# Down projection of a hybrid decoder layer: Strassen's seven products in place of the plain product

## The chip, the core and the metric

The kernel runs on one core of a Trainium2 chip. The metric is the device time of one execution in microseconds; lower is better. The engines are TensorE (PE for its matmuls, PEld for its weight loads in the profile), VectorE (DVE), ScalarE (ACT), GpSimd (POOL) and SyncE (SP, whose queue issues most of the DMAs).

## The reference

One layer of a hybrid trunk: two attention mixers, an output projection, and a SwiGLU feed-forward. Sequence 2048, width 1024, feed-forward width `D_FF` 2816, all in float32. The change is in the last product and the norm behind it:

```python
h = rmsnorm(x, g_ffn[l])
act = jax.nn.silu(jnp.einsum('bsd,df->bsf', h, w_gate[l])) * jnp.einsum('bsd,df->bsf', h, w_up[l])
x = x + jnp.einsum('bsf,fd->bsd', act, w_down[l])
...
return rmsnorm(x, g_final)
```

## The kernel before

The program has three stretches: the two mixers, then `phase3` with `project_out` (output projection and norm), `ffn_in` (gate and up) and `ffn_out` (down and final norm). The 2048 rows are `NT` = 4 token tiles of 512. A float32 operand is split in two: `hi` is the value cast to the type fp32r by ScalarE, `lo` the difference, taken by VectorE or GpSimd. A product of two operands is three matmuls (hi·hi, hi·lo, lo·hi).

`ffn_in` already uses Strassen's (Winograd's) seven products per block of gate and of up, and stores the activations by DMA in the scratch tensor `sc.act`. `ffn_out` does the plain product: for each token tile `t` and each half `hf` of the 1024 output columns it goes over `NF` = 22 chunks of 128 along `D_FF`. Per chunk there are 4 row blocks and 3 matmuls each, accumulated in four PSUM banks (`dn`). Weights are loaded and split two chunks at a time (`wraw_d`, `wh_d`, `wl_d`), the activations of a tile once for both halves (`actr`, `act`). At the end of a half the banks are added to the residual `xs` (L1162).

The order of instructions within each engine is set when the program is built, by a scheduler that knows estimated durations; on the chip each engine works through its list in order and waits on semaphores. Tiles come from pools that are stacked in SBUF; a tile laid over an older one waits for that one's last reader.

Of the kernel before, what the change touches and what calls it, by code (L numbers as in the profile page):

```python
# [113 lines left out]
def bcast_row(nc, dst, row):  # L114
    nc.sync.dma_start(dst, row.partition_broadcast(P))
# [669 lines left out]
def phase3(tc, consts, x, w_o, g_ffn, w_gate, w_up, w_down, g_final, out, sc):  # L785
    nc = tc.nc
    with ExitStack() as es:
        ps = es.enter_context(tc.tile_pool(name="ps3", bufs=8, space=PSUM, reuse_waits="tile"))
        rw = es.enter_context(tc.tile_pool(name="rw3", bufs=4, reuse_waits="tile"))
        project_out(tc, consts, ps, rw, x, w_o, g_ffn, sc)  # L790
        ffn_in(tc, ps, rw, w_gate, w_up, sc)
        ffn_out(tc, consts, ps, rw, w_down, g_final, out, sc)


def row_rstd(nc, sp, half, src, name):
    sq = sp.tile([P, D], F32, tag="sqr", name="sqr")
    ss = sp.tile([P, 1], F32, tag="ssr", name="ssr")
    nc.scalar.activation(sq, src, AF.Square, accum_out=ss)
    return rstd_of(nc, sp, ss, D, 1, half, name), sq


def project_out(tc, consts, ps, rw, x, w_o, g_ffn, sc):
# [4 lines left out]
    wov = w_o[0].rearrange("(k p) n -> p k n", p=P)  # L807
    with ExitStack() as es:
        pool = lambda name, bufs: es.enter_context(tc.tile_pool(name=name, bufs=bufs, reuse_waits="tile"))
        op, wp0, slot, xp, hp, wp1, cp, sp = (pool(n, b) for n, b in (  # L810
            ("op", 2), ("wo30", 1), ("slot", 6), ("x3", 2), ("hst", 2), ("wo31", 1), ("c3", 1), ("s3", 2)))
        wp = (wp0, wp1)
        gf = cp.tile([P, D], F32, name="gf")
        wo = {}
# [123 lines left out]
def ffn_in(tc, ps, rw, w_gate, w_up, sc):  # L938
# [2 lines left out]
    nc = tc.nc  # L941
    views = [w[0].rearrange("(k p) n -> p k n", p=P) for w in (w_gate, w_up)]
    with ExitStack() as es:
        gp = es.enter_context(tc.tile_pool(name="g3", bufs=1, reuse_waits="tile"))
        tp = es.enter_context(tc.tile_pool(name="t3", bufs=1, reuse_waits="tile"))
        ap = es.enter_context(tc.tile_pool(name="a3", bufs=1, reuse_waits="tile"))
        whl = es.enter_context(tc.tile_pool(name="whl3", bufs=9, reuse_waits="tile"))
        bufs = {"T": 6, "u": 5, "v": 3, "g": 6}
# [133 lines left out]
        for t2 in range(NT // 2):  # L1082
            w0 = weights(views[0], 0, "g")
            S = operands(t2)
            for j in range(DFF // (2 * P)):
                gate = {}

                def gated(a, b, v, psum):
                    g = tmp("g", "gate") if psum else v
                    nc.scalar.activation(g, v, AF.Silu)  # L1090
                    gate[a, b] = g

                def upped(a, b, v, psum):
                    g = gate[a, b]
                    (nc.vector if psum else nc.gpsimd).tensor_mul(g, v, g)  # L1095
                    nc.sync.dma_start(sc.act[2 * t2 + a, :, 2 * j + b, :], g)

                if j:
                    quads(S, views[0], j, "g", "g", gated)
                else:  # L1100
                    first_quads(S, w0, "g", gated)
                quads(S, views[1], j, "u", "v", upped)


def ffn_out(tc, consts, ps, rw, w_down, g_final, out, sc):
    nc = tc.nc
    half = consts[1]
    orr = out[0].rearrange("(i r) d -> r i d", r=16)
    wdv = w_down[0].rearrange("(k p) n -> p k n", p=P)
    NF = DFF // P  # L1110
    with ExitStack() as es:
        actp = es.enter_context(tc.tile_pool(name="act", bufs=29, reuse_waits="tile"))
        whl = es.enter_context(tc.tile_pool(name="wd3", bufs=4, reuse_waits="tile"))
        xp = es.enter_context(tc.tile_pool(name="x4", bufs=1, reuse_waits="tile"))
        sp = es.enter_context(tc.tile_pool(name="s4", bufs=2, reuse_waits="tile"))
        cp = es.enter_context(tc.tile_pool(name="c4", bufs=1, reuse_waits="tile"))
# [3 lines left out]
        def load_act(t, f):  # L1120

            raw = rw.tile([P, 2, 512], F32, tag="raw", name="actr")
            nc.sync.dma_start(raw, sc.act[t, :, f:f + 2, :])
            out = []
            for u in range(2):
                a = actp.tile([P, 2, 512], F32R, tag="act", name="act")
                nc.scalar.copy(a[:, 0], raw[:, u])  # L1127
                nc.gpsimd.tensor_sub(a[:, 1], raw[:, u], a[:, 0].bitcast(F32))  # L1128
                out.append(a)
            return out  # L1130

        def load_w(f, hf):
            raw = rw.tile([P, 2, 512], F32, tag="raw", name="wraw_d")
            nc.sync.dma_start(raw, wdv[:, f:f + 2, hf * 512:(hf + 1) * 512])
            wh = whl.tile([P, 2, 512], F32R, tag="wh", name="wh_d")
            nc.scalar.copy(wh, raw)  # L1136
            wl = whl.tile([P, 2, 512], F32R, tag="wl", name="wl_d")
            nc.vector.tensor_sub(wl, raw, wh.bitcast(F32))  # L1138
            return wh, wl

        def half_out(t, xs, acts, hf, tail):
            acc = [ps.tile([P, 512], F32, tag="mm", name="dn") for _ in range(4)]
            w = {}

            def step(kk, i):
                for n, (a, b) in enumerate(((0, 0), (0, 1), (1, 0))):
                    nc.tensor.matmul(acc[i], acts[kk][:, a, i * P:(i + 1) * P], w[kk // 2][b][:, kk % 2, :],  # L1147
                                     start=(kk == 0 and n == 0), stop=(kk == NF - 1 and n == 2))

            for kk in range(NF):  # L1150
                if kk % 2 == 0:
                    w[kk // 2] = load_w(kk, hf)
                if len(acts) <= kk:
                    acts += load_act(t, kk)
                if kk < NF - tail:
                    for i in range(4):
                        step(kk, i)
            for i in range(4):
                for kk in range(NF - tail, NF):
                    step(kk, i)  # L1160
                xv = xs[:, i, hf * 512:(hf + 1) * 512]
                nc.vector.tensor_add(xv, acc[i], xv)  # L1162

        def final(t, xs):
            for i in range(4):
                rs, y = row_rstd(nc, sp, half, xs[:, i, :], f"z{t}_{i}")
                nc.vector.scalar_tensor_tensor(y, xs[:, i, :], rs, gfin, op0=ALU.mult, op1=ALU.mult)
                nc.gpsimd.dma_start(orr[RES[4 * t + i]], y)

        def half_squares(xs, hf, name):  # L1170
            sq = sp.tile([P, D], F32, tag="sqr", name="sqh")
            ss = sp.tile([P, 4], F32, tag="ssh", name="ssh" + name)
            for i in range(4):
                nc.scalar.activation(sq[:, :512], xs[:, i, hf * 512:(hf + 1) * 512], AF.Square, accum_out=ss[:, i:i + 1])
            return ss

        def final_last(t, xs, s0):
            s1 = half_squares(xs, 1, "1")
            for i in range(4):
                ss = sp.tile([P, 1], F32, tag="ssr", name="ssl")  # L1180
                nc.vector.tensor_add(ss, s0[:, i:i + 1], s1[:, i:i + 1])  # L1181
                rs = rstd_of(nc, sp, ss, D, 1, half, f"zl{i}")
                y = sp.tile([P, D], F32, tag="sqr", name="yl")
                for hf in range(2):
                    cols = slice(hf * 512, (hf + 1) * 512)
                    nc.vector.scalar_tensor_tensor(y[:, cols], xs[:, i, cols], rs, gfin[:, cols], op0=ALU.mult, op1=ALU.mult)  # L1186
                    nc.sync.dma_start(orr[RES[4 * t + i]][:, cols], y[:, cols])

        for t in range(NT):
            last = t == NT - 1  # L1190
            xs = xp.tile([P, 4, D], F32, tag="xs", name=f"xo{t}")
            nc.sync.dma_start(xs, sc.x1[t])
            acts = []
            half_out(t, xs, acts, 0, 0)
            if last:
                s0 = half_squares(xs, 0, "0")
            half_out(t, xs, acts, 1, 4 if last else 0)
            if last:
                final_last(t, xs, s0)
            else:  # L1200
                final(t, xs)
# [31 lines left out]
```

## Time and profile before

| | |
|---|---|
| time, median of 3 runs | 2465.59 us (2462.58 to 2466.73) |
| time of the profiled execution | 2461.11 us |
| its span, first to last instruction | 2459.3 us |
| matmuls of `ffn_out` | 1968.97 us to 2450.40 us of the span |

A page of the profile gives busy time per engine, and can be asked for windows of time, groups of instructions by line, waits, and single instructions in order of time. A wait names the engine that waits and what ended the wait. A busy PE means that matmuls are queued back to back; the granted clock says at which of two speeds they run.

### The profile page before, as it was taken

Reading aid. Unit: us, or ns where it says so; the run is one execution under the profiler, and the core shown is the slowest. Engines: PE = TensorE matmul, PEld = TensorE weight load, DVE = VectorE, ACT = ScalarE, POOL = GpSimd, SP = SyncE. Lnnn points to the kernel's source line nnn. Section 1 sums busy time; section 2 is a strip of 40 time slices with the busy share of each in tenths; the row PEclk is TensorE's granted clock in tenths of the full one; section 3 lists DMA queues with packets and bytes.
Section 4 is the critical chain, followed back from the end, with each engine's and each line's share of the span. In section 5 each row is a group of like instructions: output and inputs, shape, how many; then the busy total and the mean of one; then the engine's idle time right before and its main releaser. Section 6 shows DMA issues by size and latency. Waiting matters only on the chain. (4 is left out here: it accounts for less than half of the span.)

```text
span 2459.3 us, 33676 instructions
## 1 busy us (share of the span) xinstructions
PE 2357.3 (96%) x12029; PEld 1999.6 (81%) x12029; DVE 1441.7 (59%) x2969; ACT 1028.2 (42%) x2361; POOL 460.6 (19%) x431
## 2 busy tenths in 40 slices
PE   7999999998999898989999999899999999999998
PEld 7987788887999776867888887688888778888887
DVE  5335554447999867669565556956655333434342
ACT  5323355554898943344332333433332232323241
POOL 2211211112111021122111012311101151414140
PEclk9999999998999899999999999999999999999999
DMA  7666566569997887843222222322222273636361
GB/s 220 210 189 209 163 180 180 145 171 245 221 221 174 240 230 202 261 159 125 86 86 86 70 95 81 126 90 88 86 69 86 71 254 120 239 122 230 127 231 60
DMA packets 250136, 384.26 MB, mean 156 GB/s; under 512 B 19681, under 2 KB 148321, under 8 KB 244465
## 3 DMA queue, kind: packets, MB, share of 16 engines
q1 hardware_dynamic: 244784, 367.03, 49.7%
q0 software_dynamic: 4896, 14.75, 2.0%
q8 instruction: 95, 1.56, 0.3%
q14 instruction: 73, 0.59, 0.1%
q10 hardware_dynamic: 288, 0.33, 0.0%
HBM read 263.43 MB, written 118.62 MB: 155 GB/s over the span
## 5 line engine op out<-in xcount | busy, mean ns | idle before, releaser
L1147 PE MATMUL dn<-wh_d,act 128*128 128x512 f32 x1408 | 435.2, 390 | 2.3 <-ACT act L1127 2.3
L1147 PEld LDWEIGHTS dn<-wh_d,act 128*128 128x128 f32 x1408 | 264.9, 188 | 58.0 <-ACT act L1127 2.7
L1138 DVE TENSOR_TENSOR wl_d<-wraw_d,wh_d 128x1024 fp32r<-128x1024 f32 x88 | 138.5, 1580 | 272.1 <-ACT wh_d L1136 272.1
L1147 PE MATMUL dn<-wl_d,act 128*128 128x512 f32 x704 | 275.1, 391 | 0.5 <-DVE wl_d L1138 0.5
L1095 POOL TENSOR_TENSOR c<-c,c 128x512 f32<-128x512 f32 x66 | 103.1, 1564 | 714.2 <-DVE c L1041 525.5
L988 ACT CAST wh<-T 128x512 fp32r<-128x512 f32 x176 | 108.9, 624 | 257.3 <-PE Yg L1023 70.7
L468 DVE TENSOR_TENSOR hl<-pt,hl 128x512 fp32r<-128x512 f32 (+1 forms) x224 | 145.2, 657 | 77.4 <-ACT hl L467 76.9
L443 ACT ACTIVATE p<-t,m 128x256 f32<-128x256 f32 (+1 forms) x384 | 176.8, 477 | 18.9 <-DVE m L668 18.9
L1128 POOL TENSOR_TENSOR act<-actr,act 128x512 fp32r<-128x512 f32 x88 | 123.5, 1424 | 255.5 <-ACT act L1127 255.3
L169 PE MATMUL acc<-hh,wh 128*128 128x512 f32 x416 | 170.2, 409 | 0.7 <-DVE vt L239 0.7
L169 PE MATMUL acc<-hh,wl 128*128 128x512 f32 x416 | 170.5, 410 | 0.0
L169 PE MATMUL acc<-hl,wh 128*128 128x512 f32 x416 | 170.2, 409 | 0.0
L885 PE MATMUL acco<-woh,oT 128*128 128x512 f32 x512 | 162.9, 396 | 1.0 <-DVE oT L857 1.0
L1136 ACT CAST wh_d<-wraw_d 128x1024 fp32r<-128x1024 f32 x88 | 91.9, 1049 | 164.3 <-PE dn L1147 143.4
L1147 PEld LDWEIGHTS dn<-wl_d,act 128*128 128x128 f32 x704 | 132.6, 188 | 28.3 <-DVE wl_d L1138 0.9
L486 PE MATMUL o<-hl,v 128*128 128x128 f32 (+1 forms) x816 | 143.3, 297 | 7.6 <-DVE hl L468 6.9
L467 ACT CAST hl<-pt 128x512 fp32r<-128x512 f32 (+1 forms) x224 | 124.8, 565 | 46.3 <-PE pt L462 45.9
L990 DVE TENSOR_TENSOR wl<-T,wh 128x512 fp32r<-128x512 f32 x176 | 122.9, 702 | 32.6 <-ACT wh L988 32.2
L462 PE MATMUL pt<-ident,p 128*128 128x128 f32 x848 | 135.7, 283 | 4.6 <-ACT p L443 2.1
L421 PE MATMUL s<-k,q 128*128 128x256 f32 (+1 forms) x768 | 122.1, 290 | 18.5 <-DMA k<-kB 8.7
L486 PEld LDWEIGHTS o<-hl,v 128*128 128x128 f32 x816 | 113.3, 196 | 11.8 <-DVE hl L468 10.4
L421 PEld LDWEIGHTS s<-k,q 128*128 128x128 f32 x768 | 100.8, 192 | 26.4 <-DVE nma L558 7.1
(453 smaller groups left out, 5509.9 us busy)
## 6 DMA issues: line engine op xcount, KB each, us to landing
wraw_d<-in_w_down_dram SPq DMA_DIRECT2D x88, 512.0 KB
wraw_g<-in_w_gate_dram SPq DMA_DIRECT2D x44, 512.0 KB
wraw_u<-in_w_up_dram SPq DMA_DIRECT2D x44, 512.0 KB
actr<-actS SPq DMA_DIRECT2D x44, 512.0 KB
actS<-c SPq DMA_DIRECT2D x68, 256.0 KB
k<-kB SPq DMA_DIRECT2D x32, 512.0 KB
xt<-in_x_dram SPq DMA_DIRECT2D x16, 512.0 KB
qA<-hia SPq DMA_DIRECT2D x32, 256.0 KB
```

Of the source, the lines that this page charges most:

```text
L169: nc.tensor.matmul(acc, a[:, k, :], mv, start=(n == 0), stop=(n == 3 * KC - 1))
L421: nc.tensor.matmul(s[:, i, :n], b["q"], b["k"][m], start=(m == 0), stop=(m == 1))
L443: nc.scalar.activation(b["pv"](p[:, i, :n]), b["tv"](b["t"]), AF.Exp, scale=-1.0, bias=nm[:, c:c + 1], accum_out=l[:, c:c + 1])
L462: nc.tensor.transpose(pt[:, sl, :], p[:, i, hfn * P:(hfn + 1) * P], ident)
L467: nc.scalar.copy(hi, pt[:, a:z, :])
L468: nc.vector.tensor_sub(lo, pt[:, a:z, :], hi.bitcast(F32))
L486: nc.tensor.matmul(out, v[:, vi, :], mov, start=(first and n == 1), stop=(last and n == 2 * len(jobs)))
L885: nc.tensor.matmul(acc, oT[kk // 2][:, kk % 2, a, i * P:(i + 1) * P], b[:, kk, :], start=(n == 0), stop=(n == 11))
L990: nc.vector.tensor_sub(lo, src, hi.bitcast(F32))
L1128: nc.gpsimd.tensor_sub(a[:, 1], raw[:, u], a[:, 0].bitcast(F32))
L1138: nc.vector.tensor_sub(wl, raw, wh.bitcast(F32))
L1147: nc.tensor.matmul(acc[i], acts[kk][:, a, i * P:(i + 1) * P], w[kk // 2][b][:, kk % 2, :], start=(kk == 0 and n == 0), stop=(kk == NF - 1 ...
```

## The change

`ffn_out` is written anew. Token tiles are taken in two pairs (`t2`), chunks in eleven pairs (`j`), output columns in two halves, so that each pair of chunks is a two by two block product, done with seven products P1 to P7 instead of eight. The eleven pairs form three groups of 4, 4 and 3; a step is one product over one group, so there are 2·3·7 = 42 steps. Each `Pair` loads tile `E` (even chunk: two activation tiles, two weight halves) and `F` (odd chunk). `operands` forms the sums of a product in place in `E`, `F` and `ST` and splits them into `o4` (tag `o`, six buffers): the activation half and the weight half side by side. `self.alt` is VectorE for even `j` and GpSimd for odd `j`.

PSUM holds three sets of four banks, X, Y and Z, out of eight banks; a later product of a set accumulates upon the earlier one, and after every step `evict` adds the set to the residual `xs`, or P1's to `a1`. At the last group the sums with `a1`, the squares and the final norm follow row block by row block. While PE does step `s`, the program lists the operands of step `s + 1` and the evictions of step `s - 1`.

The pools of `project_out`, `ffn_in` and `ffn_out` are opened in another order, so that other tiles lie upon each other, and the last four stores of activations in `ffn_in` go through GpSimd's queue instead of SyncE's.

```diff
-        op, wp0, slot, xp, hp, wp1, cp, sp = (pool(n, b) for n, b in (
-            ("op", 2), ("wo30", 1), ("slot", 6), ("x3", 2), ("hst", 2), ("wo31", 1), ("c3", 1), ("s3", 2)))
+        op, wp0, wp1, cp, sp, xp, hp, slot = (pool(n, b) for n, b in (
+            ("op", 2), ("wo30", 1), ("wo31", 1), ("c3", 1), ("s3", 2), ("x3", 2), ("hst", 2), ("slot", 6)))
...
+                    q = nc.gpsimd if t2 == NT // 2 - 1 and j == DFF // (2 * P) - 1 else nc.sync
+                    q.dma_start(sc.act[2 * t2 + a, :, 2 * j + b, :], g)
...
+    GROUPS = [range(0, 4), range(4, 8), range(8, 11)]
+    ORDER = ("P1", "P6", "P2", "P7", "P5", "P4", "P3")
...
+    BANK = {"P1": "X", "P2": "X", "P6": "Y", "P7": "Y", "P4": "Y", "P5": "Z", "P3": "Z"}
+    TO = {"P6": (0, 1), "P2": (0, 0), "P7": (1, 1), "P5": (1, 1), "P4": (1, 0), "P3": (0, 1)}
...
+        ep, fp, op, st, xp, cp, sp = (pool(n, b) for n, b in (
+            ("e4", 5), ("f4", 4), ("op4", 6), ("st4", 4), ("x4", 3), ("c4", 1), ("s4", 2)))
...
+            def split(self, src, lo):
+                o = op.tile([P, 2, 2, 512], F32R, tag="o", name="o4")
+                nc.scalar.copy(o[:, 0], src)
+                lo.tensor_sub(o[:, 1], src, o[:, 0].bitcast(F32))
+                return o
...
+                if n == "P1":
+                    o = self.split(two(self.E, 0, 3), V)
+                    self.alt.tensor_sub(two(self.E, 1, 3), two(self.E, 0, 2), two(self.E, 1, 3))
+                elif n == "P6":
+                    self.ST = st.tile([P, 2, 512], F32, tag="st", name="ST")
+                    self.alt.tensor_sub(self.ST, two(self.F, 1, 3), two(self.E, 1, 3))
+                    o = self.split(self.ST, V)
+                elif n == "P2":
+                    o = self.split(two(self.F, 0, 2), self.alt)
+                    V.tensor_sub(two(self.F, 0, 2), two(self.F, 0, 2), self.ST)
+                elif n == "P7":
+                    G.tensor_sub(self.E[:, 2], self.F[:, 3], self.E[:, 2])
+                    o = self.split(self.E[:, 1:3], V)
+                elif n == "P5":
+                    G.tensor_add(self.E[:, 0], self.E[:, 0], self.ST[:, 0])
+                    o = self.split(two(self.E, 0, 3), V)
+                elif n == "P4":
+                    o = self.split(self.F[:, 1:3], V)
+                else:
+                    o = self.split(two(self.F, 0, 3), V)
...
+            if n == "P1":
+                if g:
+                    V.tensor_add(a1[t2][:, i], src, a1[t2][:, i])
+                else:
+                    nc.scalar.copy(a1[t2][:, i], src)
+                return
+            a, hf = TO[n]
+            d = xs[t2, a][:, i, hf * 512:(hf + 1) * 512]
+            V.tensor_add(d, src, d)
+            if not end:
+                return
+            add_a1 = {"P6": (0, 1, G), "P2": (1, 1, V), "P7": (1, 0, V)}.get(n)
...
+            def cell(n, bank, ops, kk, i):
+                for m, (u, v) in enumerate(((0, 0), (0, 1), (1, 0))):
+                    nc.tensor.matmul(bank[i], ops[kk][:, u, 0, i * P:(i + 1) * P], ops[kk][:, v, 1, :],
...
+            def other(q):
+                if nxt and q < len(pairs[nxt[:2]]):
+                    made.append(pairs[nxt[:2]][q].operands(nxt[2]))
+                if s:
+                    evict(*steps[s - 1], q)
...
+            for q in range(4):
+                if q < len(ops):
+                    for i in range(4):
+                        cell(n, fresh, ops, q, i)
+                other(q)
+            banks[BANK[n]] = fresh
```

VectorE's list before, at the end of the first half of tile 0. `wl_d` are weight splits, `xo0<-dn` evictions.

```order
L1138 TENSOR_TENSOR wl_d_19226<-wraw_d_19222,wh_d_19224 128x1024
L1138 TENSOR_TENSOR wl_d_19256<-wraw_d_19252,wh_d_19254 128x1024
L1162 TENSOR_TENSOR xo0_18760<-dn_18762,xo0_18760 128x512
L1162 TENSOR_TENSOR xo0_18760<-dn_18763,xo0_18760 128x512
L1162 TENSOR_TENSOR xo0_18760<-dn_18764,xo0_18760 128x512
L1162 TENSOR_TENSOR xo0_18760<-dn_18765,xo0_18760 128x512
L1138 TENSOR_TENSOR wl_d_19286<-wraw_d_19282,wh_d_19284 128x1024
```

VectorE's list now, from P3's step of the first group into P1's of the second. L1148 is the lo part of a split, L1154 and L1157 are sums in place, L1205 evictions.

```order
L1148 TENSOR_TENSOR o4_19301<-E_19112,o4_19301 128x1024
L1157 TENSOR_TENSOR ST_19360<-F_19256,E_18828 128x1024
L1148 TENSOR_TENSOR o4_19318<-E_19116,o4_19318 128x1024
L1148 TENSOR_TENSOR o4_19335<-E_19120,o4_19335 128x1024
L1154 TENSOR_TENSOR E_19116<-E_19116 128x2x512
L1205 TENSOR_TENSOR xo00_18808<-bZ_19124,xo00_18808 128x512
L1157 TENSOR_TENSOR ST_19396<-F_19264,E_19116 128x1024
L1148 TENSOR_TENSOR o4_19362<-ST_19360,o4_19362 128x1024
L1205 TENSOR_TENSOR xo00_18808<-bZ_19125,xo00_18808 128x512
L1205 TENSOR_TENSOR xo00_18808<-bZ_19126,xo00_18808 128x512
L1205 TENSOR_TENSOR xo00_18808<-bZ_19127,xo00_18808 128x512
```

Where an eviction of a half stood behind 11 weight splits, evictions now come every four to eight sums or splits, and the first two sums of the next product stand ahead of them.

GpSimd's list before, at the final norm of tile 0 (L1128 splits of activations, L110 the power of the norm, L1168 stores).

```order
L1128 TENSOR_TENSOR act_19728<-actr_19726,act_19728 128x512
L1128 TENSOR_TENSOR act_19731<-actr_19726,act_19731 128x512
L110 TENSOR_TENSOR rs_z0_0_19531<-ms_z0_0_19529,half_81 128x1
L110 TENSOR_TENSOR rs_z0_1_19540<-ms_z0_1_19538,half_81 128x1
L1168 DMA out_0_dram<-sqr_19526 128x1024
L1168 DMA out_0_dram<-sqr_19535 128x1024
```

GpSimd's list now, at the final norm of tile 1, in which the second pair of tiles has begun.

```order
L110 TENSOR_TENSOR rs_z011_20287<-ms_z011_20285,half_81 128x1
L1157 TENSOR_TENSOR ST_20452<-F_20231,E_20097 128x1024
L1163 TENSOR_TENSOR E_20097<-F_20231,E_20097 128x512
L1166 TENSOR_TENSOR E_20093<-E_20093,ST_20422 128x512
L110 TENSOR_TENSOR rs_z012_20316<-ms_z012_20314,half_81 128x1
L1166 TENSOR_TENSOR E_20097<-E_20097,ST_20452 128x512
L110 TENSOR_TENSOR rs_z013_20333<-ms_z013_20331,half_81 128x1
L1148 TENSOR_TENSOR o4_20503<-F_20223,o4_20503 128x1024
```

The power of the norm, which stood behind two splits of 512, now stands between sums of 1024 and 512 that themselves wait for loads and for VectorE.

## Rows read from the trace of the kernel before

**Rows 1.** The page, busy time by engine over the whole span.

```profile
PE 2357.3 (96%) x12029; PEld 1999.6 (81%) x12029; DVE 1441.7 (59%) x2969; ACT 1028.2 (42%) x2361; POOL 460.6 (19%) x431
```

**Rows 2.** Windows: from:to, length, busy by engine (count), granted clock, DMA share, GB/s.

```profile
1969.00:2450.00 481.00, 480.54 (x2111) 397.39 (x2112) 175.71 (x150) 153.40 (x211) 139.77 (x115) 1.00 0.51 173
2100.00:2120.00 20.00, 20.00 (x90) 16.54 (x90) 10.81 (x9) 9.42 (x14) 11.42 (x11) 1.00 0.94 336
1966.00:1972.00 6.00, 3.73 (x12) 2.41 (x10) 4.04 (x3) 2.18 (x4) 4.58 (x4) 0.78 0.69 246
1972.00:1978.00 6.00, 6.00 (x26) 4.96 (x26) 0.00 (x0) 0.00 (x0) 3.71 (x3) 0.93 0.99 406
```

**Rows 3.** Groups by line, 1850 to 2460 us: busy, mean ns | idle before.

```profile
L1147 PE MATMUL dn<-wh_d,act 128*128 128x512 f32 x1408 | 435.2, 390 | 2.3 <-ACT act L1127 2.3
L1147 PE MATMUL dn<-wl_d,act 128*128 128x512 f32 x704 | 275.1, 391 | 0.5 <-DVE wl_d L1138 0.5
L1138 DVE TENSOR_TENSOR wl_d<-wraw_d,wh_d 128x1024 fp32r<-128x1024 f32 x88 | 138.5, 1580 | 272.1 <-ACT wh_d L1136 272.1
L1136 ACT CAST wh_d<-wraw_d 128x1024 fp32r<-128x1024 f32 x88 | 91.9, 1049 | 164.3 <-PE dn L1147 143.4 <-DMA wraw_d<-in_w_down_dram 8.3 <-PE Yu L1023 5.5
```

**Rows 4.** PE's waits, 1300 to 2459 us: total, times, longest.

```profile
PE dn L1147 <- ACT act L1127: 2.3, 1, 2.3
PE dn L1147 <- DVE wl_d L1138: 0.5, 1, 0.5
```

**Rows 5.** Single lines of the stage: duration in ns, minimum/median/maximum.

```profile
L1138 DVE TENSOR_TENSOR wl_d<-wraw_d,wh_d x88: 1211/1226/2304, 1967.4 to 2429.8; 128x1024 fp32r<-128x1024 f32 x88
L1162 DVE TENSOR_TENSOR xo<-dn,xo x32: 674/691/692, 2029.5 to 2450.8; 128x512 f32<-128x512 f32 x32
L1128 POOL TENSOR_TENSOR act<-actr,act x88: 1274/1296/2318, 1969.7 to 2375.8; 128x512 fp32r<-128x512 f32 x88
```

**Rows 6.** VectorE in order of time: start, duration, instruction, count.

```profile
1091.52 1.89 DVE L990 TENSOR_TENSOR wl<-T,wh 128x512 fp32r<-128x512 f32 x3
...
1108.96 1.79 DVE L967 TENSOR_TENSOR S2l<-s,S2h 128x512 fp32r<-128x512 f32 x1
1110.67 1.78 DVE L967 TENSOR_TENSOR S1l<-s,S1h 128x512 fp32r<-128x512 f32 x1
1112.38 1.78 DVE L967 TENSOR_TENSOR S3l<-s,S3h 128x512 fp32r<-128x512 f32 x1
```

**Rows 7.** GpSimd in order of time, the same stretch.

```profile
1108.46 1.74 POOL L967 TENSOR_TENSOR A12l<-hraw,A12h 128x512 fp32r<-128x512 f32 x1 [3.10 <-ACT A12h L966]
1110.16 1.74 POOL L967 TENSOR_TENSOR A22l<-hraw,A22h 128x512 fp32r<-128x512 f32 x1
1111.87 1.74 POOL L977 TENSOR_TENSOR s<-hraw 128x512 f32<-128x512 f32 x1
```

**Rows 8.** GpSimd in order of time, 878 to 890 us.

```profile
879.13 9.91 POOL L824 TENSOR_TENSOR wol<-wraw_o,woh 128x1024 fp32r<-128x1024 f32 x4 [92.21 <-ACT woh L823]
```

**Rows 9.** VectorE in order of time, the same stretch.

```profile
883.86 2.92 DVE L848 TENSOR_TENSOR ob<-ob 128x512 f32<-128x512 f32 x1 [5.02 <-DMA ob<-oA]
...
889.51 0.68 DVE L848 TENSOR_TENSOR ob<-ob 128x512 f32<-128x512 f32 x1
```

**Rows 10.** PE in order of time, where `ffn_out` begins.

```profile
1966.31 0.39 PE L1023 MATMUL Zu<-S4l,wh 128*128 128x512 f32 x1
1968.97 0.50 PE L1147 MATMUL dn<-wh_d,act 128*128 128x512 f32 x1 [2.27 <-ACT act L1127]
...
1969.63 0.63 PE L1147 MATMUL dn<-wh_d,act 128*128 128x512 f32 x1
1970.06 0.63 PE L1147 MATMUL dn<-wl_d,act 128*128 128x512 f32 x1
```

**Rows 11.** All engines in order of time, the end.

```profile
2450.01 0.39 PE L1147 MATMUL dn<-wh_d,act 128*128 128x512 f32 x1
...
2451.00 0.54 POOL L110 TENSOR_TENSOR rs_zl<-ms_zl,half 128x1 f32<-128x1 f32 x1 [1.66 <-DVE ms_zl L108]
2452.36 1.41 DVE L1186 SCALAR_TENSOR_TENSOR yl<-xo,rs_zl,gfin 128x512 f32<-128x512 f32 x2 [0.90 <-POOL rs_zl L110]
2454.75 1.42 DVE L1186 SCALAR_TENSOR_TENSOR yl<-xo,rs_zl,gfin 128x512 f32<-128x512 f32 x2 [0.72 <-POOL rs_zl L110]
```

More of the change, by code (lines that the diff above doesn't have):

```diff
@@ L788, in phase3 @@
         ps = es.enter_context(tc.tile_pool(name="ps3", bufs=8, space=PSUM, reuse_waits="tile"))
[L789 to L792, printed above, removed]
+        with tc.tile_pool(name="rw3", bufs=4, reuse_waits="tile") as rw:
+            project_out(tc, consts, ps, rw, x, w_o, g_ffn, sc)
+            ffn_in(tc, ps, rw, w_gate, w_up, sc)
+        ffn_out(tc, consts, ps, w_down, g_final, out, sc)
 def row_rstd(nc, sp, half, src, name):
@@ L943, in ffn_in @@
     with ExitStack() as es:
[L944 to L948, printed above, removed]
+        pool = lambda name, bufs: es.enter_context(tc.tile_pool(name=name, bufs=bufs, reuse_waits="tile"))
+        tp, ap, gp, vp, whl, up = (pool(n, b) for n, b in (
+            ("t3", 6), ("a3", 1), ("g3", 6), ("v3", 3), ("whl3", 9), ("u3", 5)))
+        temps = {"T": tp, "g": gp, "v": vp, "u": up}
         def tmp(tag, name):
-            return (gp if tag == "g" else tp).tile([P, 512], F32, tag=tag, name=name, bufs=bufs[tag])
+            return temps[tag].tile([P, 512], F32, tag=tag, name=name)
         def operands(t2):
@@ L1095, in upped @@
                     (nc.vector if psum else nc.gpsimd).tensor_mul(g, v, g)
-                    nc.sync.dma_start(sc.act[2 * t2 + a, :, 2 * j + b, :], g)
+                    q = nc.gpsimd if t2 == NT // 2 - 1 and j == DFF // (2 * P) - 1 else nc.sync
+                    q.dma_start(sc.act[2 * t2 + a, :, 2 * j + b, :], g)
                 if j:
@@ L1102, in ffn_in, with ffn_out @@
                 quads(S, views[1], j, "u", "v", upped)
-def ffn_out(tc, consts, ps, rw, w_down, g_final, out, sc):
+def ffn_out(tc, consts, ps, w_down, g_final, out, sc):
     nc = tc.nc
@@ L1109, in ffn_out @@
     wdv = w_down[0].rearrange("(k p) n -> p k n", p=P)
-    NF = DFF // P
-    with ExitStack() as es:
[L1112 to L1116, printed above, removed]
-        gfin = cp.tile([P, D], F32, name="gfin")
-        bcast_row(nc, gfin, g_final)
[L1120 to L1155, printed above, removed]
-                    for i in range(4):
[L1157 to L1201, printed above, removed]
```

94 lines of the change are left out of this document (added).

## Prediction

> **What bounds the kernel now.** I first read the page and the windows. Over the whole span PE is busy 96% and VectorE 59% [rows 1]; what counts here is the stretch of `ffn_out`, where PE is busy 480.5 of 481.0 us, VectorE 175.7, ScalarE 153.4, GpSimd 139.8 [rows 2]. Next the groups by line and PE's waits: 1408 + 704 = 2112 matmuls of 512 columns, with 2.3 and 0.5 us of waiting [rows 3, 4]. So this stretch is bound by the number of matmuls and nothing else. From the first matmul at 1968.97 to the end of the last at 2450.01 + 0.39 it is 481.4 us [rows 10, 11], or 0.228 us for each. The other engines have slack: VectorE's 88 weight splits sat idle 272 us before them, waiting for ScalarE's casts, and those waited 143 us for PE to free buffers [rows 3].
>
> **What the change removes.** Seven products over eleven pairs, two pairs of tiles, 4 row blocks and 3 matmuls are 7·11·2·12 = 1848 matmuls, 264 fewer. At 0.228 us that is **-60.2 us**, if PE never waits. The price lies on the engines that form and split the operands, and a step of four pairs now lasts only 48·0.228 = 10.9 us, a step of three 36·0.228 = 8.2 us.
>
> **VectorE's new work.** I counted its list for the new stage: 190 sums and splits of 1024 elements, 160 evictions of 512 out of PSUM, 16 sums of 512 with `a1`, 32 scalings of 512. Three sums of 512 in a row take 1.89 us and the last 0.69 of it, so they follow each other every 0.60 us; an eviction alone lasts the same 0.69 [rows 5, 6], so I give it 0.60. A split of 1024 lasts 1.23 us alone (the median, [rows 5]); with the same 0.09 us of overlap it is 1.14. Two scalings last 1.41 us [rows 11], 0.70 each. Sum: 190·1.14 + 160·0.60 + 16·0.60 + 32·0.70 = 216.6 + 96.0 + 9.6 + 22.4 = 344.6 us, against 420.9 us of PE. By itself it would fit.
>
> **What GpSimd does to VectorE.** The 88 splits have a median of 1.23 us, a maximum of 2.30 [rows 5] and a mean of 1.58 [rows 3]. The reason stands in the two lists from 1108 to 1114 us: both engines have work all the time, and each gets one instruction per 1.70 us, VectorE's with a duration of 1.78 instead of 0.69 and GpSimd's 1.74 instead of 1.30 [rows 5 to 7]. They take turns. One GpSimd instruction of 512 thus costs VectorE 1.70 - 0.60 = 1.10 us. One of 1024 (four in 9.91 us, 2.48 each) held a VectorE sum of 512 for 2.92 us instead of 0.68, a cost of 2.24 [rows 8, 9]. Evictions out of PSUM are not held: their maximum is 0.692 [rows 5]. The new list of GpSimd has 30 instructions of 1024 and 52 of 512, so 30·2.24 + 52·1.10 = **124 us** for which it can hold VectorE. 344.6 + 124.4 = 469 us would be above PE's 420.9. How much of it arrives depends on how often VectorE wants two SBUF operands at that moment; I take its own share of such work in each step.
>
> The Trainium skill speaks against this change at the same place (page "SBUF — State Buffer", section "Who interferes with whom"): a VectorE instruction with two SBUF inputs and a GpSimd instruction that reads SBUF exclude each other for the whole instruction. By that rule the hold is GpSimd's whole duration, 30·2.48 + 52·1.30 = 142 us instead of 124; the trace agrees but for about 0.2 us per instruction.
>
> **Step by step.** During a step of four pairs VectorE does four evictions (2.4 us) and the sums and splits of the next product.
> - Making P1, P6 or P2: six of 1024, 6.8 + 2.4 = 9.2 us, beside two GpSimd instructions of 1024; 6.8/9.2 = 0.74 of them arrive, 2·2.24·0.74 = 3.3. Together 12.5, over PE's 10.9 by 1.6.
> - Making P7 or P5: four of 1024, 7.0 us, beside four GpSimd sums of 512, 4·1.10·0.65 = 2.9. Together 9.9.
> - Making P4 or P3: 7.0.
>
> A group of four is 3·12.5 + 2·9.9 + 2·7.0 = 71.3 us against 76.3 of PE. The excess of 3·1.6 = 4.8 us stands in three steps in a row. The lists leave room for about that much: a set of banks is not written again for a whole step after its end, the eviction needs 2.4 us of it, and six `o4` buffers are one and a half steps. I take 0 us lost in the four groups of four; without that room it is 4·4.8 = 19.
>
> The two groups of three: a step is 8.2 us, still with four evictions. Making P6 is 5·1.14 + 2.4 + 1.6 = 9.7 (over by 1.5). Making P2 is 9.7 and the eight sums with `a1`, 4.8, which the scheduler put here: 14.5 (over by 6.3). Making P7 is 3.4 + 2.4, and seven GpSimd instructions of 512 (three sums, four with `a1`) at 1.10·0.59: 10.3 (over by 2.1). Together 9.9, of which the room takes 5. **+5 us** for each group, +10; between 4 and 20.
>
> The border between the two pairs of tiles: in the last step of three and the next of four (19.1 us of PE) VectorE makes P1 and P6 of four pairs, 25 us, and finishes eight row blocks, 8·(2·0.70 + 0.4 for the small ones, an estimate) = 14. Over by 20, less 5 of room. On GpSimd the power of the norm (0.54 us, [rows 11]) now stands behind sums of 1024 and 512, as its list shows, and the scalings behind it on VectorE wait too; three such instructions of GpSimd are 2.48 + 2·1.30 = 5 us, and half of it is covered: 3. **+18 us**; between 8 and 25.
>
> At the first group of each pair ScalarE copies P1's banks before it casts `ST`, and PE needs that cast: three copies and a cast of 1.05 us [rows 3] behind P1's end, some 2 us, twice: **+4 us** (0 to 6). ScalarE is otherwise free: four casts per step, 4.2 of 10.9 us.
>
> The clock: at the start of `ffn_out` PE stood 2.27 us idle, and its matmuls then came every 0.43 us instead of 0.23 [rows 10]; the granted clock is 0.78 and 0.93 in the two windows of 6 us [rows 2], so 6·0.22 + 6·0.07 = 1.7 us went at the half clock of 1.2 GHz. In the places above I expect four or five such stalls, in part hidden while VectorE is late anyway: **+4 us** (0 to 8).
>
> **Loads.** `F` has four tiles for four pairs, so the next group's can only be loaded when P3's splits are made, and must be there within the next step but one. That is 4 MB in some 29 us, 140 GB/s. The queue has moved 336 and 406 GB/s in windows [rows 2]: nothing added; below 140 it would cost about 5 us per group.
>
> **Ends.** Start: before, PE lost 2.3 us idle and 1.7 us of clock. Now the last stores of activations no longer stand before the first loads in SyncE's queue: -2 (-4 to +3). End: two row blocks of two tiles end together, one eviction of 0.60 and one finish of 1.41 and its power more: +2.5 (0 to 5). The pools of the two earlier functions move instructions only a few places: 0 (-5 to +5).
>
> **Sum.** -60.2 + 10 + 18 + 4 + 4 - 2 + 2.5 = -23.7 us. Against the profiled execution's own 2461.1 that is 2437.4. The runs have a median 4.5 us higher, 2465.6, so 2441.9 from there; I say **2440**, with 2428 to 2452 as this case's own range.
>
> **Rivals.**
> - PE stays the bound nearly everywhere: GpSimd's instructions fall beside evictions (96 us of them, not held) and the room takes the rest. Then the terms 10 and 18 shrink to 4 and 8, the clock's to 0: -60.2 + 16 = -44, with -2 and -4 from ends and order about 2412. For it: 71.3 against 76.3 in the groups of four. Against: the border, which no room covers.
> - Every GpSimd instruction holds VectorE in full (the exclusion that the skill's page states, with nothing beside it). Then making P1, P6, P2 is 13.7, P7 and P5 11.4, a group of four 78: 3 us late each, 12 with what the room can't take; the groups of three 9 each, the border 22, ScalarE and clock 10: 62 us, no change, 2455 to 2468. For it: both lists are nearly always full. Against: VectorE spends 30% of its time on evictions and waits.
> - Slower: PE loses its clock at the heavy steps. A stall of 2.3 us with 1.7 us of half clock behind it is 4.0 us, and 60.2/4.0 = 15 such stalls use up the gain. There are 18 heavy steps (three in each of six groups) and two at the border; if all stall so, 80 us, +20, 2481. For it: 12.5 against 10.9 in each. Against: one excess of 1.6 us is short of the 2.27 that preceded the slow clock here.
>
> **How the numbers follow.** Chances: forecast 0.46, PE bound 0.25, full hold 0.15, slow clock 0.14. The predicted time is the forecast's. The range takes in most of the second and the third and reaches toward the fourth: 2408 to 2476, leaving out about 0.08 below and 0.12 above. A measurement here can tell 0.2%, some 5 us. Faster by that: all of the first two, half of the third: 0.78. Same: 0.10, from the third and the edge of the fourth. Slower: 0.12.
>
> **What would show it.** 1848 matmuls with about 0.23 us each and, in the windows of the last group of either pair and of the border, PE below 90% busy, its waits ended by VectorE (evictions and `o4`). VectorE busy some 430 us in the stage, its 1024 forms with a mean near 1.6 us and a median near 1.2; GpSimd busy about 150. PE full in the groups of four. Wrong would be: waits of PE ended by DMA (`F`), a granted clock under 0.95 through the stage, or stalls spread over all groups.

## The result and the profile after

The changed kernel takes **2445.54 us** (median of 5 runs, 2443.37 to 2454.77), the kernel before on the same chip 2465.8 (5 runs, 2462.58 to 2468.62): a ratio of 0.9924, 95% interval 0.9902 to 0.9946, so 20 us faster. The forecast was 2440, with 2428 to 2452 as the range of its own case. The number came out right; its terms did not all. The profiled execution took 2443.37 us with a span of 2441.6, which is 17.7 less than before.

The page of the changed kernel, busy time by engine, which answers to [rows 1]:

```profile
PE 2312.3 (95%) x11765; PEld 1949.7 (80%) x11765; DVE 1702.8 (70%) x3239; ACT 1054.3 (43%) x2371; POOL 531.5 (22%) x417
```

264 matmuls are gone and 45 us of PE's busy time; VectorE has 261 us more. Where the stage pays is seen in its windows, cut at the first matmul of a step (columns as in [rows 2]):

```profile
1964.10:2000.20 36.10, 26.89 (x98) 19.74 (x97) 24.34 (x15) 11.00 (x14) 31.52 (x16) 0.91 0.64 255
2000.20:2065.40 65.20, 65.20 (x289) 54.00 (x288) 60.57 (x54) 23.39 (x23) 22.68 (x10) 1.00 0.38 129
2065.40:2088.70 23.30, 22.36 (x97) 17.87 (x97) 21.68 (x17) 9.91 (x10) 16.84 (x7) 1.00 0.00 1
2088.70:2140.40 51.70, 51.70 (x229) 42.79 (x228) 46.94 (x47) 18.74 (x18) 15.47 (x7) 1.00 0.47 163
2140.40:2179.00 38.60, 34.64 (x145) 26.48 (x144) 38.57 (x40) 15.76 (x22) 13.92 (x7) 1.00 0.22 77
2179.00:2206.20 27.20, 27.20 (x121) 22.52 (x120) 26.47 (x27) 12.62 (x24) 15.16 (x8) 1.00 0.37 123
2206.20:2255.50 49.30, 39.73 (x146) 30.24 (x145) 49.30 (x57) 19.75 (x27) 27.02 (x15) 0.86 0.45 156
2255.50:2299.00 43.50, 43.50 (x194) 36.02 (x193) 37.47 (x33) 14.76 (x14) 18.23 (x8) 1.00 0.47 162
...
sum 465.00, PE 436.38 PEld 350.11 DVE 427.53 ACT 177.37 POOL 209.02; mean PE 36.36 PEld 29.18 DVE 35.63 ACT 14.78 POOL 17.42
```

Where PE is full, 228 matmuls take 51.70 us: 0.2267 for each. The length of a window less its matmuls at this price is what it loses. The first two steps (96 matmuls, 21.8 us) lose **14.3**; P6 and P2 of the second group (23.30 for 96) lose 1.5; P6 to P5 of the group of three (38.60 for 144) lose 6.0; the border between the pairs (49.30 for 144) loses **16.7**, all else nothing. The second pair's later groups repeat the first's within 0.2. The stage is 465.0 us from its first matmul to the end of its last, 46.0 over 1848·0.2267.

PE's waits in the stage (as [rows 4]):

```profile
PE bY L1254 <- DVE o L1148: 9.4, 6, 4.7
PE bY L1254 <- ACT o L1147: 6.6, 3, 3.4
PE bY L1254 <- DVE xo L1205: 4.8, 8, 1.3
PE bX L1254 <- DVE o L1148: 4.0, 6, 1.1
PE bX L1254 <- DVE a L1199: 2.8, 4, 0.8
PE bZ L1254 <- DVE xo L1205: 1.1, 2, 0.5
```

Operands (`o`) are late for 20.0 us, evictions (`xo`, `a`) for 8.7; no wait of PE is ended by a load. VectorE's and GpSimd's groups in the stage (busy, mean ns | idle before; answers to [rows 3] and [rows 5]):

```profile
L1148 DVE TENSOR_TENSOR o<-E,o 128x1024 fp32r<-128x1024 f32 x66 | 99.3, 1528 | 0.7 <-ACT o L1147 0.7
L1154 DVE TENSOR_TENSOR E<-E 128x1024 f32<-128x1024 f32 x12 | 26.5, 2204 | 0.1
...
L1166 POOL TENSOR_TENSOR E<-E,ST 128x512 f32<-128x512 f32 x22 | 42.2, 1927 | 1.2 <-DVE ST L1157 1.2
L1154 POOL TENSOR_TENSOR E<-E 128x1024 f32<-128x1024 f32 x10 | 32.1, 3208 | 9.5 <-DVE o L1148 9.5
```

VectorE's 190 forms of 1024 have a mean of 1.61 us and a median of 1.22, as forecast. But GpSimd's are held as well: 3.21 us instead of the 2.48 of [rows 8], its sums of 512 1.93 instead of 1.30.

Now the first group itself, in order of time. PE, then GpSimd, then one line of VectorE and ScalarE's:

```profile
1978.56 1.19 PE L1254 MATMUL bY<-o 128*128 128x512 f32 x4 [1.20 <-ACT o L1147]
1980.92 2.11 PE L1254 MATMUL bY<-o 128*128 128x512 f32 x8 [1.17 <-DVE o L1148]
1986.42 7.28 PE L1254 MATMUL bY<-o 128*128 128x512 f32 x24 [3.40 <-ACT o L1147]
1995.70 1.39 PE L1254 MATMUL bY<-o 128*128 128x512 f32 x4 [2.00 <-ACT o L1147]
```

```profile
1975.24 3.29 POOL L1154 TENSOR_TENSOR E<-E 128x1024 f32<-128x1024 f32 x1 [2.30 <-DVE o L1148]
1978.49 1.29 POOL L1163 TENSOR_TENSOR E<-F,E 128x512 f32<-128x512 f32 x1
1979.74 2.26 POOL L1166 TENSOR_TENSOR E<-E,ST 128x512 f32<-128x512 f32 x1
1981.97 3.32 POOL L1157 TENSOR_TENSOR ST<-F,E 128x1024 f32<-128x1024 f32 x1
1985.25 3.51 POOL L1163 TENSOR_TENSOR E<-F,E 128x512 f32<-128x512 f32 x2
1988.72 3.52 POOL L1166 TENSOR_TENSOR E<-E,ST 128x512 f32<-128x512 f32 x2
1992.20 2.37 POOL L1157 TENSOR_TENSOR ST<-F,E 128x1024 f32<-128x1024 f32 x1
```

```profile
1975.09 1.21 DVE L1157 TENSOR_TENSOR ST<-F,E 128x1024 f32<-128x1024 f32 x1
```

```profile
1976.00 1.56 ACT L1201 COPY a<-bX 128x512 f32<-128x512 f32 x3 [11.48 <-PE bX L1254]
1977.43 1.07 ACT L1147 CAST o<-ST 128x1024 fp32r<-128x1024 f32 x1
...
1985.32 1.99 ACT L1147 CAST o<-ST 128x1024 fp32r<-128x1024 f32 x2 [6.33 <-POOL ST L1157]
1994.61 1.04 ACT L1147 CAST o<-ST 128x1024 fp32r<-128x1024 f32 x1 [7.29 <-POOL ST L1157]
```

At the pauses of 3.40 and 2.00 us PE waits for ScalarE's cast, and the cast for a sum `ST` on GpSimd that ends at 1985.3 and 1994.6. The waits call the releaser ScalarE; one step further back it is GpSimd, late with the results that it makes itself. The first pause, 1.20, is another: VectorE's `ST` ends at 1976.30, and its cast starts only at 1977.43, behind three of ScalarE's copies.

The granted clock, in windows cut where it falls:

```profile
1986.30:1989.70 3.40, 3.28 (x8) 2.61 (x9) 3.30 (x2) 1.01 (x2) 3.40 (x3) 0.50 1.05 449
1996.60:2000.00 3.40, 3.40 (x10) 2.66 (x9) 3.37 (x3) 3.40 (x5) 3.40 (x2) 0.51 0.02 5
2215.00:2221.80 6.80, 4.82 (x11) 3.80 (x12) 6.80 (x10) 3.35 (x6) 5.25 (x4) 0.50 0.23 85
2242.30:2249.10 6.80, 6.18 (x15) 4.83 (x16) 6.80 (x9) 1.05 (x1) 0.00 (x0) 0.50 0.43 158
```

Each stretch at 1.2 GHz follows PE's pauses in the first group or at the border. In the windows above that costs (1 - 0.91)·36.1 + (1 - 0.86)·49.3 = 10 us of the 31 lost there.

At the start PE no longer waits before its first matmul, but its first step of 14.5 us, 3.6 over its matmuls, still pauses 1.08 for an operand. The last matmul ends at 2429.05, 12.55 us before the span's end (8.9 before).

### The profile page after: what moved, and what is told of

Read it like the earlier page. It is cut to its first block, busy times and chain, and to the rows that moved or that the text cites. A ratio compares the mean times of both kernels' runs of the same rounds, so it can differ in the third digit from the quotient of the medians.

```text
span 2441.6 us, 33440 instructions
## 1 busy us (share of the span) xinstructions
PE 2312.3 (95%) x11765; PEld 1949.7 (80%) x11765; DVE 1702.8 (70%) x3239; ACT 1054.3 (43%) x2371; POOL 531.5 (22%) x417
## 4 chain that ended last, share of the span: by engine, by line
PE 43%; DVE 10%; issue 3%; DMA 3%; POOL 2%; ACT 1%; SPq 0%; DVEq 0%; POOLq 0%; ACTq 0%
PE Yu L1022 7%; PE Yg L1022 7%; PE Zu L1022 5%; PE Xu L1022 5%; PE Zg L1022 4%; PE Xg L1022 4%; PE bY L1254 3%; PE acco L885 3%; DVE o L1148 3%; PE bZ L1254 2%; PE bX L1254 1%; DVE xo L1205 1%; DVE xo L1192 1%; DMA E<-in_w_down_dram 1%; DVE F L1161 1%
## 5 line engine op out<-in xcount | busy, mean ns | idle before, releaser
L1254 PE MATMUL bY<-o 128*128 128x512 f32 x792 | 195.5, 403 | 20.8 <-DVE o L1148 9.4
L1254 PEld LDWEIGHTS bY<-o 128*128 128x128 f32 x792 | 152.6, 195 | 60.7 <-DVE o L1148 11.9
L989 DVE TENSOR_TENSOR wl<-T,wh 128x512 fp32r<-128x512 f32 x176 | 124.5, 712 | 17.0 <-ACT wh L987 16.7
L1254 PE MATMUL bX<-o 128*128 128x512 f32 x528 | 125.4, 393 | 6.7 <-DVE o L1148 4.0
L1254 PEld LDWEIGHTS bX<-o 128*128 128x128 f32 x528 | 98.7, 189 | 31.5 <-DVE o L1148 6.8
L1254 PE MATMUL bZ<-o 128*128 128x512 f32 x528 | 122.7, 389 | 1.1 <-DVE xo L1205 1.1
L885 PEld LDWEIGHTS acco<-woh,oT 128*128 128x128 f32 x512 | 97.2, 190 | 26.0 <-ACT oT L856 4.1
L425 DVE CUSTOM_DVE_ANT_0 t<-s,tab 128x256 f32<-128x256 f32 (+1 forms) x344 | 112.9, 369 | 5.7 <-PE s L421 2.7
```

The costliest lines, as they stand in the source:

```text
L425: nc.vector.tensor_tensor_reduce(out=b["kv"](t[:, i, :n]), in0=b["kv"](s[:, i, :n]), in1=b["tab"], scale=-0.125, scalar=init, op0=ALU.add, ...
L885: nc.tensor.matmul(acc, oT[kk // 2][:, kk % 2, a, i * P:(i + 1) * P], b[:, kk, :], start=(n == 0), stop=(n == 11))
L989: nc.vector.tensor_sub(lo, src, hi.bitcast(F32))
L1254: nc.tensor.matmul(bank[i], ops[kk][:, u, 0, i * P:(i + 1) * P], ops[kk][:, v, 1, :], start=(n in ("P1", "P6", "P5") and kk == 0 and m == ...
```

## Experiments

Three theories. **A**: each GpSimd instruction costs VectorE the hold of the prediction (1.10 us for 512, 2.24 for 1024), more than it would take to do the work itself (0.60, 1.14). **B**: VectorE with all of it becomes the bound. **C**: it is the order of GpSimd's list in the first group, where `ST` stands behind sums of 512 that nobody needs yet. The kernel before took 2461.48 us beside all_v, st_v, sums_v and pools, and 2462.81 beside the other four. Up to the output projection all kernels have the same instructions, and yet its first matmul stands anywhere from 873.5 to 883.6 us in the ten profiles. So stages, from first matmul to the end of the last, compare more finely than spans; each is one profile. An instruction moved to another engine changes the order of both lists too, so no run here changes the holds alone.

**all_v**: GpSimd has no sums or splits of the new stage.

```diff
-                self.t2, self.j, self.alt = t2, j, G if j % 2 else V
+                self.t2, self.j, self.alt = t2, j, V
-                    G.tensor_sub(self.E[:, 2], self.F[:, 3], self.E[:, 2])
+                    V.tensor_sub(self.E[:, 2], self.F[:, 3], self.E[:, 2])
-                    G.tensor_add(self.E[:, 0], self.E[:, 0], self.ST[:, 0])
+                    V.tensor_add(self.E[:, 0], self.E[:, 0], self.ST[:, 0])
-            add_a1 = {"P6": (0, 1, G), "P2": (1, 1, V), "P7": (1, 0, V)}.get(n)
+            add_a1 = {"P6": (0, 1, V), "P2": (1, 1, V), "P7": (1, 0, V)}.get(n)
```

> Every sum and split that GpSimd had in the new stage (30 of 1024 elements, 52 of 512) goes to VectorE; the arithmetic is the same. Theory A (the two engines exclude each other, and GpSimd's list is late): nothing holds VectorE any more, so its work is 344.6 + 30*1.14 + 52*0.60 = 410 us and its 1024 forms have a mean of 1.22 us, not 1.53. A step that makes P1, P6 or P2 is 8*1.14 + 2.4 = 11.5 us instead of 12.5. The loss of PE in the stage falls from 46 us to about 24 (first group 14 to 3, groups of four 1.5 to 1, groups of three 6 to 4 each, border of the pairs 17 to 13): 2424 us. Rival B (GpSimd relieves VectorE, which is too full): VectorE gains 65 us of work against 421 of PE and is late in every step, loss 60 us or more: 2460 us.

Measured: **2421.26 us** (2419.34 to 2425.86), 0.9842 of before (0.982 to 0.9864). Its windows of the whole stage, of the first two steps and of the border, then PE's two longest waits, then groups of VectorE:

```profile
1971.70:2405.00 433.30, 423.66 (x1849) 347.14 (x1847) 405.55 (x492) 180.38 (x221) 18.94 (x14) 1.00 0.35 122
...
1971.70:2000.20 28.50, 24.61 (x98) 18.86 (x97) 28.09 (x28) 11.43 (x14) 3.25 (x3) 0.94 0.83 323
...
2199.70:2238.00 38.30, 33.87 (x146) 26.72 (x145) 37.92 (x56) 15.81 (x17) 12.61 (x6) 1.00 0.47 166
```

```profile
PE bY L1254 <- DVE o L1148: 5.2, 4, 2.2
PE bY L1254 <- ACT o L1147: 1.7, 1, 1.7
```

```profile
L1148 DVE TENSOR_TENSOR o<-E,o 128x1024 fp32r<-128x1024 f32 x66 | 79.5, 1216 | 0.1
L1154 DVE TENSOR_TENSOR E<-E 128x1024 f32<-128x1024 f32 x22 | 27.8, 1262 | 0.1
```

The stage falls from 465.0 to 433.3 us and its loss from 46.0 to 14.3; the first two steps lose 6.7, the border 5.7. VectorE does 82 instructions more and is busy 406 us instead of 427: 344.6 + 30·1.14 + 52·0.60 = 410 by the prediction's own prices. The 1024 forms are down to a mean of 1.22 us, as expected. A fits, B falls. But A's 24 us of loss were 14.3, and place by place the expectation missed: the first group kept 6.7 (3 expected), the groups of three 0.9 and 1.1 (4 each), the border 5.7 (13). The medians are 20 to 24 us apart (by ratios and as they stand) where the stages are 31.7 apart. Between the two profiles the rest is the stretch before the stage, which is 7.5 us later here at the output projection; why the medians follow it is open. So the expected 2424 was met by two misses that cancel.

**st_v** and **sums_v**: the ten sums `ST` alone, and the 44 sums of 512 alone.

```diff
-                    self.alt.tensor_sub(self.ST, two(self.F, 1, 3), two(self.E, 1, 3))
+                    V.tensor_sub(self.ST, two(self.F, 1, 3), two(self.E, 1, 3))
```

```diff
-                    G.tensor_sub(self.E[:, 2], self.F[:, 3], self.E[:, 2])
+                    V.tensor_sub(self.E[:, 2], self.F[:, 3], self.E[:, 2])
-                    G.tensor_add(self.E[:, 0], self.E[:, 0], self.ST[:, 0])
+                    V.tensor_add(self.E[:, 0], self.E[:, 0], self.ST[:, 0])
```

> Only the ten sums ST of GpSimd (line 1157) go to VectorE. Theory C (the order of GpSimd's list is the main loss: ST for a later pair stands behind the sums of P7 and P5, and PE waits for it): the first group loses about 4 us instead of 14, the border about 10 instead of 17, the rest the same: 2429 us. Theory A without the order (only the time for which GpSimd holds VectorE counts): ten holds of 2.24 less, ten sums of 1.14 more, some 11 us of VectorE's 427, of which half or less reaches PE: 2440 us.

> Only the 44 sums of 512 for P7 and P5 (lines 1163 and 1166) go from GpSimd to VectorE. Theory C (order of GpSimd's list): ST no longer stands behind them, so the first group loses about 5 us instead of 14 and the border about 9 instead of 17: 2428 us. Theory A without the order: 44 holds of 1.10 less and 44 sums of 0.60 more, 22 us of VectorE's time, mostly in steps that have slack: 2440 us.

Measured: st_v 2443.92 us (0.9934, 0.9913 to 0.9955), stage 461.0; sums_v 2438.48 us (0.9905, 0.9882 to 0.9927), stage 452.9. By ratios st_v can't be told from the changed kernel (0.9924), and sums_v hardly. With `ST` off GpSimd the first two steps and the next still lose 14.1 us (C: 4) and the border 12.9 (C: 10); in sums_v they lose 11.9 (C: 5) and 9.4 (C: 9). Both engines of st_v in the first group, GpSimd then VectorE:

```profile
1992.97 2.25 POOL L1163 TENSOR_TENSOR E<-F,E 128x512 f32<-128x512 f32 x1
1995.18 2.25 POOL L1166 TENSOR_TENSOR E<-E,ST 128x512 f32<-128x512 f32 x1
```

```profile
1991.80 4.51 DVE L1157 TENSOR_TENSOR ST<-F,E 128x1024 f32<-128x1024 f32 x2
1996.23 4.50 DVE L1148 TENSOR_TENSOR o<-ST,o 128x1024 fp32r<-128x1024 f32 x2
```

A sum of 512 on GpSimd and one of 1024 on VectorE go in turn, one of each per 2.22 us: the hold of 1.10 and VectorE's own 1.14. C falls as the main loss of the first group: the order can be mended, the taking of turns stays. At the border sums_v comes out as C has it, and there the two theories are not told apart.

**elo_v**: the third piece, the sums of `E`, P2's lo parts and the sums with `a1`.

```diff
-                    self.alt.tensor_sub(two(self.E, 1, 3), two(self.E, 0, 2), two(self.E, 1, 3))
+                    V.tensor_sub(two(self.E, 1, 3), two(self.E, 0, 2), two(self.E, 1, 3))
-                    o = self.split(two(self.F, 0, 2), self.alt)
+                    o = self.split(two(self.F, 0, 2), V)
-            add_a1 = {"P6": (0, 1, G), "P2": (1, 1, V), "P7": (1, 0, V)}.get(n)
+            add_a1 = {"P6": (0, 1, V), "P2": (1, 1, V), "P7": (1, 0, V)}.get(n)
```

> GpSimd keeps the ten ST sums and the 44 sums of 512; the ten sums of E, the ten lo parts of P2 and the eight sums of 512 with a1 go to VectorE (the pieces that all_v moved and st_v and sums_v did not). If the pieces simply add, this one is worth what is left of all_v's gain: 24.3 - 1.6 - 7.1 = 15.6 us, a time near 2430, with a loss of the stage over its matmuls near 30 us instead of 46. If the gain comes only once GpSimd is out of the way altogether (what VectorE gets back in one place is taken by the next GpSimd instruction in line), this one gives 2 to 6 us like the others, 2439 to 2444, and the three pieces together fall short of 24.

Measured: 2426.44 us (0.9859, 0.9837 to 0.988), stage 444.2. The pieces take 4.0, 12.1 and 20.8 us off the stage, together 36.9 where all at once take 31.7: they do not fall short, and overlap by 5. In times it is 1.6 + 7.1 + 19.1 = 27.8 against 24.3 by medians; by ratios it is about 18 against 20, so the times do not settle it.

**first_v**: GpSimd out of the first group alone.

```diff
-                self.t2, self.j, self.alt = t2, j, G if j % 2 else V
+                self.t2, self.j = t2, j
+                self.half = V if (t2, j // 4) == (0, 0) else G
+                self.alt = self.half if j % 2 else V
...
-                    G.tensor_sub(self.E[:, 2], self.F[:, 3], self.E[:, 2])
+                    self.half.tensor_sub(self.E[:, 2], self.F[:, 3], self.E[:, 2])
-                    G.tensor_add(self.E[:, 0], self.E[:, 0], self.ST[:, 0])
+                    self.half.tensor_add(self.E[:, 0], self.E[:, 0], self.ST[:, 0])
```

> Only the first group of the first pair of token tiles has no GpSimd sums or splits; everything behind it is as in the changed kernel. If GpSimd's 1024 sums, 3.3 us each beside VectorE's, are what makes the first group late, its loss of 14.3 us falls to the 6.7 of all_v, and the time to about 2438. If the first group is late because its operands have to be made from nothing on whichever engine, the loss stays near 14 and the time near 2445.

Measured: 2438.55 us (0.9897, 0.988 to 0.9914). Its windows of the first two steps and of the border:

```profile
1971.00:1999.20 28.20, 23.37 (x98) 17.69 (x97) 27.83 (x28) 11.39 (x14) 3.23 (x3) 1.00 0.83 325
2205.30:2252.90 47.60, 38.10 (x146) 29.24 (x145) 47.60 (x56) 19.64 (x27) 26.89 (x15) 0.89 0.44 153
```

28.20 less 96·0.2267 is 6.4 instead of 14.3; the clock there stays at 1.00. GpSimd's work made some 8 of the 14 us; the 6.4 that stay are left to the beginning from nothing, and no run takes them apart. The border, where GpSimd works as before, still loses 15.0.

**no_norm0**: the squares and the final norm of the first pair left out.

```diff
-            if n in ("P2", "P5", "P4", "P3"):
+            if n in ("P2", "P5", "P4", "P3") and t2:
                 square(t2, a, hf, i)
             if n in ("P4", "P3"):
-                finish(t2, a, i)
+                if t2:
+                    finish(t2, a, i)
+                else:
+                    for hf in range(2):
+                        cols = slice(hf * 512, (hf + 1) * 512)
+                        nc.sync.dma_start(orr[RES[8 * t2 + 4 * a + i]][:, cols], xs[t2, a][:, i, cols])
```

> The changed kernel with the squares and the final norm of the first pair of token tiles left out (their rows are stored unnormed). By the forecast's working the border between the pairs is over by 20 us of VectorE time of which 14 are the finish: the loss there falls from 16.6 to 2 to 5 us, the time to 2432 to 2434. The rival: the border loses for the same reason as the first group, GpSimd's sums of 1024 and 512 beside VectorE's while P6 and P7 are made; then some 10 us stay and the time is near 2439.

Measured: 2434.64 us (0.9887, 0.9871 to 0.9902). The border's window of 144 matmuls:

```profile
2211.60:2247.80 36.20, 33.49 (x145) 26.77 (x144) 30.49 (x28) 16.61 (x19) 17.70 (x8) 1.00 0.19 66
```

36.20 - 32.6 = 3.6 us lost instead of 16.7, as expected. With the norm go ScalarE's squares and GpSimd's powers, so the run does not tell VectorE's scalings from the waits on the powers. all_v loses 5.7 there with the norm left in. So neither the finish nor GpSimd's work alone is the cause: either one taken away saves 11 to 13 of the 16.7 us.

**all_v_a1**: all_v, and P1's first banks copied to `a1` by VectorE.

```diff
-                    nc.scalar.copy(a1[t2][:, i], src)
+                    V.tensor_copy(a1[t2][:, i], src)
```

> all_v with the first copies of P1's banks into a1 on VectorE instead of ScalarE (eight evictions of 512). The forecast had +4 us for ScalarE's copies standing ahead of its cast of ST: if that term is real, 2 to 4 us come off all_v's 2421, 2417 to 2419. If it is covered by VectorE's own list, 2421; and if VectorE is what is late there, its 4 more evictions of 0.6 us cost up to 2.4 us each time, 2421 to 2426.

Measured: 2423.06 us (2418.83 to 2428.97; 0.9841, 0.9819 to 0.9863), no gain: by ratios it is the same as all_v. Its profile is of its slowest execution; there the stage is 439.9 against all_v's 433.3. The pause before P6's first matmul in all_v and then here, and VectorE's list here:

```profile
1986.52 1.20 PE L1254 MATMUL bY<-o 128*128 128x512 f32 x4 [1.72 <-ACT o L1147]
```

```profile
1988.51 1.21 PE L1254 MATMUL bY<-o 128*128 128x512 f32 x4 [0.69 <-ACT o L1147]
```

```profile
1987.89 2.48 DVE L1201 COPY a<-bX 128x512 f32<-128x512 f32 x4
```

Without the copies ahead of it the first cast of `ST` comes sooner, and the pause falls from 1.72 to 0.69: ScalarE's copies cost PE about 1 us, once. But VectorE's 2.48 us stand before the second `ST`, and PE then waits 4.18 us for a split.

**pools**: the kernel before, with only `project_out`'s and `ffn_in`'s pools in the new order.

```diff
-            ("op", 2), ("wo30", 1), ("slot", 6), ("x3", 2), ("hst", 2), ("wo31", 1), ("c3", 1), ("s3", 2)))
+            ("op", 2), ("wo30", 1), ("wo31", 1), ("c3", 1), ("s3", 2), ("x3", 2), ("hst", 2), ("slot", 6)))
```

> The kernel before with the new order of the pools of the two earlier functions alone; the old down projection. If the pools carry part of the gain (the new kernel's first matmul of the last stage is 4.9 us earlier), this is 2 to 4 us faster than before, 2462 us, with the pause of 2.27 us at the start of the last stage kept. If the earlier start comes from the new down projection and its loads, the same as before, within 1 us.

Measured: 2474.93 us (1.0049, 1.003 to 1.0068), 0.5% slower. PE where `ffn_out` begins:

```profile
1975.24 2.07 PE L1146 MATMUL dn<-wh_d,act 128*128 128x512 f32 x4 [2.47 <-ACT wh_d L1135]
1984.53 0.80 PE L1146 MATMUL dn<-wl_d,act 128*128 128x512 f32 x1 [7.21 <-DVE wl_d L1137]
```

2.5 and 7.2 us of waiting where before had 2.3 [rows 10]. Neither branch of the expectation has this. The old `ffn_out` meets a worse start on the restacked pools, and the new one has no such wait. What the new `ffn_out` would do on the old pools, or with the last stores in SyncE's queue, no run here shows.

## Why the prediction was right

Term by term, in the profiled executions:

| term | forecast, us | measured, us |
|---|---|---|
| 264 matmuls fewer | -60.2 | -59.9 (264·0.2267) |
| second groups of four | 0 | +3.0 (1.5 each) |
| groups of three | +10 | +12.1 |
| border, with its ScalarE copies | +18 +2 | +16.7 |
| start and first group, with ScalarE's copies | -2 +2 | +9.4 (14.3, less before's 4.9) |
| clock beside these | +4 | within the rows above (10) |
| end | +2.5 | +3.6 |
| all before the stage | 0 | -2.4 |
| sum | -23.7 | -17.5 (of 17.7) |

Before's 4.9 is what the 484.1 us from the start of the last matmul of `ffn_in` to the end of the last of all have over 2112·0.2267 and the last one's 0.39 [rows 10, 11]. The row before the stage is no more than the ten profiles differ among themselves.

The number of matmuls, VectorE's busy time (430 forecast, 427 measured), the groups of three and the border were right in size, and no_norm0 shows that the finish is needed to overfill the border. By the prediction's own test, PE below 90% busy in the groups of three and at the border, with waits ended by VectorE, the windows agree.

At these two places the size is in part luck. By the prediction's prices the groups of three without GpSimd would still lose 4 us each and the border 13; all_v measures 0.9, 1.1 and 5.7. GpSimd's share was priced too low there, and what VectorE loses by its own list too high; the two errors cancel. That the lists leave more room than the 5 us taken would explain the second, but no run measures the room.

**The step that was mis-sized** is the group of four at the very start. The forecast gave it 0 for VectorE's excess, +2 for "three copies and a cast", and -2 for the start, and it measured +9.4. It priced GpSimd's work only as a hold upon VectorE. It then said "GpSimd busy about 150"; it was 209. The exclusion works both ways, so with VectorE's list full a GpSimd sum of 1024 lasts 3.2 us, and a chain of E sum, `ST`, cast and split that goes through GpSimd comes late at PE, with no step of lead yet to cover it. first_v shows what GpSimd's work costs there: 8 of 14 us. It takes the hold and the late results away together, and st_v, which moves only `ST`, still loses 14.1, with VectorE's `ST` held in turn; how the 8 us divide between the two is not shown. The ScalarE term of +4 was about 1: the pause of 1.20 in the first group is its, the casts behind the pauses of 3.40 and 2.00 were late because `ST` was, and at the border no wait of PE is ended by ScalarE.

The clock was mis-sized too, 10 us of slow matmuls where 4 were given, though part of it lies in time in which VectorE would have been late anyway.

The rivals: PE stays bound (2412) fails by the border and the first group, yet all_v comes within 10 us of it; full hold (2455 to 2468) fails: of the 124 us of hold some 427.5 - 344.6 = 83 arrived (and its 3 us late in each group of four are 77.9 - 76.3 = 1.6 by its own figures); slow clock at each heavy step (2481) fails: the clock fell in two places only.

The Trainium skill's rule (page "SBUF — State Buffer", section "Who interferes with whom") that the two engines exclude each other for the whole instruction agrees with the row of 2.22 us per pair but for about 0.2 us, since whole durations would give 1.30 + 1.14 = 2.44. The rule names no engine that goes first, and should have been read in both directions.

## What to carry to other kernels

Price a sum on a helper engine twice: what it holds the busy engine up, and how late its own result comes when it is held in turn; here 1.10 us against 0.60 and 2.24 against 1.14 said beforehand that VectorE would do better alone, even at the share of 0.65 to 0.74 of the hold that the prediction let arrive. No version here is faster than all_v, at 2421 us. In it the gain in matmuls is given back mostly where the other engines have no lead, at the first group and where one tile's finish meets the next one's beginning (6.7 and 5.7 of 14.3 us). And pools restacked for a new stage must be judged with that stage.

## What was not expected of the hardware

Even the power of the norm, 128x1 on GpSimd, is held: 0.54 us alone [rows 11], 1.19 on the mean of its 16 in the changed stage. And taking 82 instructions over made VectorE less busy, by 22 us in the stage.
